# A transformer block on one core: the output projection as seven products of halves, with weight sums kept in DRAM

## The chip, the core and the metric

The kernel runs on one core of a Trainium2 chip. The core has a matrix engine (TensorE, "PE" in the profile; its weight loads are listed apart as "PEld"), a vector engine (VectorE, "DVE"), a scalar engine (ScalarE, "ACT"), GpSimd ("POOL") and a queue that issues transfers (SyncE, "SP"). Each engine works through its own list of instructions in order; the engines wait for each other by semaphores. Matrix products are written to PSUM, eight banks of 128 partitions x 512 float32; everything else lives in SBUF, 128 partitions wide, or in DRAM, reached by DMA. The metric is the device time of one execution in microseconds (us), lower is better. Of the kernel before, three runs are shown beside one profiled execution.

## What is computed

One layer, 512 tokens, model width 2048, 16 heads of 128 (8 stick-breaking, 8 forgetting), inner width 8192, all float32:

```python
h = rmsnorm(x, g_attn)
proj = h @ w_in                              # q, k, v of both kinds of heads, forget gates
o_sb = stick_breaking_attention(qa, ka, va)
o_fox = forgetting_attention(qf, kf, vf, log_f)
mixed = concat(head_rmsnorm(o_sb, g_out_sb), head_rmsnorm(o_fox, g_out_fox))   # (512, 2048)
x = x + mixed @ w_out                        # the output projection, (2048, 2048)
h2 = rmsnorm(x, g_mlp)
x = x + relu(h2 @ w_up) ** 2 @ w_down
y = rmsnorm(x, g_final)
```

## The kernel before

A float32 product is made of three matmuls on split operands. Each operand is split into a high part (a cast on ACT, line 60) and a low part (a subtraction on DVE, line 61); `mm3` (lines 93 to 95) multiplies high by high, high by low and low by high. So each piece of weights costs one pass of ACT, one of DVE, and then PE.

Weights pass through three raw buffers (tag `wraw`, 512 KB each), issued on SP's queue, and then through three pairs of split buffers (`wh`, `wl`, from `hi_lo`). `load_w` does both.

The stages stand in this order. The projections and attention: heads in the order forgetting 6, 7, 0 to 5, then stick-breaking 0 to 7, two heads in a round (`for n in range(0, 2 * NH, 2)`). A round projects q and k of two heads (`project_q`, PSUM tile `accq`), in some rounds v (`accumulate_v`, `accv`), then runs the attention of both at a high priority (`weigh` and the functions that call it; tiles `s`, `pt`, `o`, for the last head `oq`). The normalized head goes to `mixed` (line 265), a tile of 16 heads x 512 tokens; while x is being transposed at the start the same tile holds x, and until the stick-breaking heads come its first eight slices are free.

Output projection (lines 466 to 500): four column blocks `n` of 512. For each, pairs of heads are split again from `mixed` into `uh`, `ul`; 512 KB of `w_out` are loaded and split, and 24 matmuls of 512 columns follow, into four PSUM banks `acco`, one for each block of 128 tokens. Then x is added (line 484), the sum is transposed on PE (line 489) and scaled to `hr` (491), stored to DRAM (`xd`, 492), and the left operands of the next stage are formed and split (`a_form`, lines 449 to 462, tiles `F`, written as `fh` and `fl`); the squares of the row sums go to ACT (line 500).

The up projection and the down projection already use seven products in place of eight for a 2 x 2 product of blocks (a Strassen-Winograd scheme): the sums of the left blocks are `a_form`, those of the right blocks are subtractions in `Unit.product` (lines 547 to 554) and `second`. A unit is a pair of blocks of the inner width; its weights are loaded as two transfers of 1 MB (line 536), for the first unit partly as two of 512 KB (line 531).

The order of instructions on each engine is not the order of the text. A scheduler fixes it when the program is built: it goes through the program with a model of time, takes what is ready in that model, earlier text (or a raised priority) first, and hands out buffers. The chip then keeps that order on each engine and on SP's queue, whatever arrives when. A tile pool that is closed gives its place to later pools; with `reuse_waits="tile"` the later tile waits only for the tiles that lay in its place.

## Time and profile before

| what | value |
|---|---|
| median of three runs | 2092.24 us (2091.91 to 2093.44) |
| profiled execution | 2091.42 us, its span 2089.7 us |
| granted TensorE clock, mean | 0.998 |
| DMA, whole span | 339.68 MB, mean 163 GB/s |
| attention and its projections | to about 658 us |
| output projection, first and last `acco` matmul | 626.0 and 811.4 us |
| up projection starts | 813.35 us |

The profile gives, for one execution, each engine's busy time, the chain of work that ended last (followed back from the last instruction), groups of instructions by source line and tile ("L61 DVE ... wl<-wraw,wh" is line 61 on DVE, which writes `wl` from `wraw` and `wh`), with their count, busy time, mean in ns and the idle time of the engine before them, and on request the same for any stretch of time, in order of time, or by wait. "[0.91 <-DVE fl L61]" behind a row says that the engine was idle 0.91 us before it and what ended that. Busy times of matmuls overlap, since matmuls are pipelined.

### The profile page before, as it was taken

Reading aid. Unit: us, or ns where it says so; the run is one execution under the profiler, and the core shown is the slowest. Engines: PE = TensorE matmul, PEld = TensorE weight load, DVE = VectorE, ACT = ScalarE, POOL = GpSimd, SP = SyncE. Lnnn points to the kernel's source line nnn. Section 1 sums busy time; section 2 is a strip of 40 time slices with the busy share of each in tenths; the row PEclk is TensorE's granted clock in tenths of the full one; section 3 lists DMA queues with packets and bytes.
Section 4 is the critical chain, followed back from the end, with each engine's and each line's share of the span. In section 5 each row is a group of like instructions: output and inputs, shape, how many; then the busy total and the mean of one; then the engine's idle time right before and its main releaser. Section 6 shows DMA issues by size and latency. Waiting matters only on the chain.

```text
span 2089.7 us, 29877 instructions
## 1 busy us (share of the span) xinstructions
PE 2071.5 (99%) x12096; PEld 1842.0 (88%) x12096; DVE 1570.9 (75%) x1746; ACT 1036.4 (50%) x1399; POOL 50.7 (2%) x76
## 2 busy tenths in 40 slices
PE   9999999999999999999999999999999999999998
PEld 8888888888898888999999999999888888888886
DVE  5454545665676666888888888888798888989895
ACT  6333334444445655556665656666743343433443
POOL 0000000000000000000000000000000000000003
PEclk9999999999999999999999999999999999999999
DMA  6333322323323434466566566567856664764732
GB/s 193 81 90 82 85 87 74 88 80 82 81 81 114 157 133 151 137 207 192 182 222 186 186 202 204 182 196 246 298 201 238 232 232 170 288 218 159 264 119 81
DMA packets 239930, 339.68 MB, mean 163 GB/s; under 512 B 7936, under 2 KB 154416, under 8 KB 233776
## 3 DMA queue, kind: packets, MB, share of 16 engines
q1 hardware_dynamic: 238832, 335.64, 49.3%
q8 instruction: 95, 1.56, 0.3%
q10 hardware_dynamic: 960, 2.13, 0.3%
q14 instruction: 43, 0.35, 0.0%
HBM read 272.20 MB, written 65.54 MB: 162 GB/s over the span
## 4 chain that ended last, share of the span: by engine, by line
PE 96%; DVE 2%; DMA 1%; ACT 1%; issue 0%; ACTq 0%; SPq 0%
PE accd L93 7%; PE accd L94 7%; PE accd L95 7%; PE psa L93 6%; PE psa L94 6%; PE psa L95 6%; PE accq L95 6%; PE accq L94 6%; PE accq L93 6%; PE psc L94 3%; PE psc L95 3%; PE psc L93 3%; PE acco L95 3%; PE acco L93 3%; PE acco L94 3%; PE accv L93 3%
## 5 line engine op out<-in xcount | busy, mean ns | idle before, releaser
L60 ACT CAST wh<-wu 128x1024 fp32r<-128x1024 f32 x164 | 171.0, 1048 | 138.7 <-PE psa L94 54.7
L61 DVE TENSOR_TENSOR wl<-wu,wh 128x1024 fp32r<-128x1024 f32 x164 | 199.4, 1221 | 46.5 <-ACT wh L60 46.2
L60 ACT CAST wh<-wd 128x1024 fp32r<-128x1024 f32 (+1 forms) x136 | 134.9, 999 | 184.5 <-PE accd L95 112.8
L61 DVE TENSOR_TENSOR wl<-wraw,wh 128x1024 fp32r<-128x1024 f32 (+2 forms) x133 | 158.6, 1193 | 84.7 <-ACT wh L60 84.1
L93 PE MATMUL psa<-fh,wh 128*128 128x256 f32 x776 | 220.2, 284 | 1.1 <-ACT s L563 1.1
L94 PE MATMUL psa<-fl,wh 128*128 128x256 f32 x776 | 220.0, 284 | 0.9 <-DVE fl L61 0.9
L95 PE MATMUL psa<-fh,wl 128*128 128x256 f32 x776 | 219.8, 283 | 0.0
L60 ACT CAST wh<-wraw 128x1024 fp32r<-128x1024 f32 (+2 forms) x133 | 135.4, 1019 | 154.3 <-PE accq L94 68.5
L93 PE MATMUL accq<-hH,wh 128*128 128x512 f32 x512 | 200.5, 392 | 0.0
L95 PE MATMUL accq<-hH,wl 128*128 128x512 f32 x512 | 200.3, 391 | 0.0
L94 PE MATMUL accq<-hL,wh 128*128 128x512 f32 x512 | 200.2, 391 | 0.0
L61 DVE TENSOR_TENSOR wl<-wd,wh 128x1024 fp32r<-128x1024 f32 (+1 forms) x136 | 155.4, 1153 | 37.6 <-ACT wh L60 37.1
L93 PE MATMUL accd<-wh,uf 128*128 128x512 f32 x436 | 169.7, 389 | 0.9 <-issue 0.9
L94 PE MATMUL accd<-wl,uf 128*128 128x512 f32 x436 | 169.6, 389 | 0.0
L95 PE MATMUL accd<-wh,uf 128*128 128x512 f32 x436 | 169.6, 389 | 0.0
L93 PEld LDWEIGHTS psa<-fh,wh 128*128 128x128 f32 x776 | 149.4, 192 | 1.6 <-ACT s L563 1.3
L94 PEld LDWEIGHTS psa<-fl,wh 128*128 128x128 f32 x776 | 149.3, 192 | 1.2 <-DVE fl L61 1.1
L95 PEld LDWEIGHTS psa<-fh,wl 128*128 128x128 f32 x776 | 149.2, 192 | 0.0
L60 ACT CAST wx<-wd 128x1024 fp32r<-128x1024 f32 (+1 forms) x88 | 87.4, 999 | 114.1 <-PE accd L95 69.9
L61 DVE TENSOR_TENSOR wx<-wd,wx 128x1024 fp32r<-128x1024 f32 (+1 forms) x88 | 100.9, 1152 | 22.9 <-ACT wx L60 22.4
L94 PEld LDWEIGHTS accq<-hL,wh 128*128 128x128 f32 x512 | 96.2, 188 | 19.6
L95 PEld LDWEIGHTS accq<-hH,wl 128*128 128x128 f32 x512 | 96.2, 188 | 19.3
(306 smaller groups left out, 5505.8 us busy)
## 6 DMA issues: line engine op xcount, KB each, us to landing
wu<-in_w_up_dram SPq DMA_DIRECT2D x63, 1024.0 KB, 6.4
ufd<-st SPq DMA_DIRECT2D x98, 512.0 KB, 6.7
wd<-in_w_down_dram SPq DMA_DIRECT2D x48, 1024.0 KB, 6.9
wraw<-in_w_in_dram SPq DMA_DIRECT2D x84, 512.0 KB, 3.7
uf<-ufd SPq DMA_DIRECT2D x42, 1024.0 KB, 7.1
wraw<-in_w_out_dram SPq DMA_DIRECT2D x32, 512.0 KB, 3.5
wd<-in_w_down_dram SPq DMA_DIRECT2D x16, 768.0 KB, 6.8
uf<-ufd SPq DMA_DIRECT2D x14, 768.0 KB, 6.4
```

What stands on the lines that cost most here:

```text
L60: ins = act.copy(hi, src)
L61: lows[0] = dve.tensor_tensor(lo, src, hi.bitcast(F32), op=ALU.subtract)
L93: pe.matmul(out, sh, mh, start=first, stop=False, skip_group_check=True)
L94: pe.matmul(out, sh, ml, start=False, stop=False, skip_group_check=True)
L95: pe.matmul(out, sl, mh, start=False, stop=last, skip_group_check=True)
```

## The change

The output projection becomes seven products of halves too: the 2048 x 2048 weights are cut into 2 x 2 blocks (rows by even and odd head, columns by half), the attention output into 2 x 2 blocks (tokens by half, heads by even and odd).

1. The sums of the weight blocks: in each of the first four rounds of heads, two slices (256 rows of `w_out` each, 2 MB) are loaded into the free half of `mixed`, four subtractions on DVE make the four sums, and 2 MB are stored to DRAM (`wsums`, 16 MB in all). Products 5, 7, 4 and 6 later read their weights there, products 1, 2 and 3 from `w_out`.
2. The left operands `G` of the seven products are formed from `mixed` by the same `a_form` as in the next stage, whole (256 tokens x 8 pairs of heads), in 14 tiles: eight of them lie where the transposed input `hH`, `hL` lay (now eight tiles `h4` in the pool `form1`).
3. For each of two column blocks `db` the products run in the order 1, 2, 5, 6, 7, 3, 4 over four pieces of weights each; sums go into three pairs of PSUM banks A, B, C, and `take` adds them to four quarters of x (`x2`). Products 1 and 2 of the first block begin with the pieces that need no late head (4, 6, 0).
4. A quarter of x that is complete is turned at once (`turn_quarter`); the left operands `F` of the up projection are formed by `left_form` in quarters, in the second block into rooms that `G` has left.
5. At the end of the stage, the weights of units 0 and 1 are loaded, and products 1 and 2 of unit 0 and product 1 of unit 1 are put ahead of the forms that need the last quarter.

The diff, cut to its core:

```diff
+            def sums_of_weights(m):
+                b = mixed[:, :NH].rearrange("p (q a) n -> p q (a n)", a=2)
+                sp.dma_start(b.rearrange("p (s j) c -> p s j c", s=2),
+                             w_out[2 * m * P:2 * (m + 1) * P].rearrange("(s p) (j c) -> p s j c", s=2, j=2))
+                b11, b12, b21, b22 = (b[:, i] for i in range(4))
+                dve.tensor_tensor(b11, b12, b11, op=ALU.subtract)
+                dve.tensor_tensor(b12, b22, b12, op=ALU.subtract)
+                dve.tensor_tensor(b22, b22, b11, op=ALU.subtract)
+                dve.tensor_tensor(b21, b21, b22, op=ALU.subtract)
+                sp.dma_start(wsums[:, m], b)
...
                 qk = [project(0), project(1)]
+                if n < NH:
+                    sums_of_weights(n)
+                    sums_of_weights(n + 1)
...
-    for n in range(4):
-        ns = slice(n * NT, (n + 1) * NT)
-        ps = [acc.tile([P, NT], F32, tag="acc", name="acco") for _ in range(TB)]
...
-            for t in range(TB):
-                ts = slice(t * P, (t + 1) * P)
-                for i in range(2):
-                    mm3(ps[t], ms[i][0][:, ts], ms[i][1][:, ts], *w[i], k0 + i == 0, k0 + i == 2 * NH - 1)
...
+    def g_form(p, m0, m1):
+        a_form(p, mixed[:, 2 * m0:2 * m1].rearrange("p (m s) n -> p m s n", s=2), [g[:, m0:m1, :] for g in G[p]], S_OF[:, m0:m1, :])
+
+    def out_piece(p, db, m0):
+        raw = wp.tile([P, 2, NT], F32, tag="wraw", name="wo")
+        cols = slice(db * NT, (db + 1) * NT)
+        if p in (1, 2, 3):
+            i, j = {1: (0, 0), 2: (1, 0), 3: (1, 1)}[p]
+            sp.dma_start(raw, out_rows[i][:, m0:m0 + 2, j * 2 * NT:(j + 1) * 2 * NT][:, :, cols])
+        else:
+            sp.dma_start(raw, wsums[:, m0:m0 + 2, {5: 0, 7: 1, 4: 2, 6: 3}[p], cols])
+        hi, lo = (w.rearrange("p (a b) -> p a b", a=2) for w in hi_lo(2 * NT))
+        split(hi, lo, raw)
+        ps = {2: B, 5: C, 3: C}.get(p, A)
+        for t in range(2):
+            ts = slice(t * P, (t + 1) * P)
+            for i in range(2):
+                mm3(ps[:, t, :], G[p][0][:, m0 + i, ts], G[p][1][:, m0 + i, ts], hi[:, i, :], lo[:, i, :],
+                    m0 + i == 4 and p in (1, 5, 2), m0 + i == 3)
...
+    def take(p):
+        for q, ps in {1: [((0, 0), A)], 5: [((1, 1), C)], 6: [((0, 1), A)], 2: [((0, 0), B)], 7: [((1, 1), A)],
+                      3: [((0, 1), C)], 4: [((1, 0), A)]}[p]:
+            for t in range(2) if p in (4, 6) else [slice(0, 2)]:
+                dve.tensor_tensor(x2[q][:, t, :], x2[q][:, t, :], ps[:, t, :], op=ALU.add)
...
+    for db in range(2):
+        begin(0, 0, db)
+        if db == 0:
+            for p in (1, 2):
+                g_form(p, 4, 8)
+                g_form(p, 0, 2)
+                for m0 in (4, 6, 0):
+                    out_piece(p, db, m0)
+            for p in (1, 2):
+                g_form(p, 2, 4)
+            for p in (5, 6, 7, 3, 4):
+                g_form(p, 4, 8)
+                g_form(p, 0, 2)
+                g_form(p, 2, 4)
+            mixp_cm.__exit__(None, None, None)
+            rw = ctx.enter_context(tc.tile_pool(name="rw", bufs=5, side="right", reuse_waits="tile"))
+        for i, p in enumerate(G_ORDER):
+            for m0 in (2,) if db == 0 and p in (1, 2) else (4, 6, 0, 2):
+                out_piece(p, db, m0)
...
+            take(p)
+            if db == 1:
+                for q in A_ORDER[2 * i:2 * i + 2]:
+                    for j in range(2):
+                        left_form(q, 0, j)
...
+            if p in (2, 7, 3):
+                turn_quarter(*{2: (0, 0), 7: (1, 1), 3: (0, 1)}[p], db)
+            if db == 1 and p == 6:
+                units = [Unit(u) for u in range(2)]
...
+        if db == 1:
+            begun = [units[0].parts(1), units[0].parts(2)]
+        turn_quarter(1, 0, db)
...
+    for p in (1, 2):
+        units[0].multiply(p, begun[p - 1])
+    units[0].finish(1)
+    begun.append(units[1].parts(1))
+    left_form(4, 1, 0)
+    left_form(5, 1, 0)
+    units[1].multiply(1, begun[2])
+    left_form(6, 1, 0)
+    for p in (7, 3):
+        left_form(p, 1, 1)
+        left_form(p, 1, 0)
```

The pools `acc`, `u`, `att`, `attp` and `mix` get `reuse_waits="tile"`.

## The prediction

> **What bounds the kernel now.** I read the engine totals, then the chain of work that ended last, then busy time by stretch.

> ```profile
> span 2089.7 us, 29877 instructions
> PE 2071.5 (99%) x12096; PEld 1842.0 (88%) x12096; DVE 1570.9 (75%) x1746; ACT 1036.4 (50%) x1399; POOL 50.7 (2%) x76
> PE 96%; DVE 2%; DMA 1%; ACT 1%; issue 0%; ACTq 0%; SPq 0%
> ```

> PE is 96% of the chain, so removed matmuls come off the end as long as everything else stays hidden behind PE. The stretches (columns: length; busy PE, weight loads, DVE, ACT, POOL with counts; clock, DMA share, GB/s):

> ```profile
> 200.00:300.00 100.00, 100.00 (x467) 83.79 (x466) 60.09 (x95) 38.25 (x64) 3.56 (x6) 1.00 0.30 81
> 626.00:680.00 54.00, 54.00 (x259) 45.30 (x258) 37.02 (x50) 28.95 (x46) 0.89 (x2) 1.00 0.34 118
> 680.00:812.00 132.00, 132.00 (x603) 109.39 (x602) 84.54 (x113) 74.22 (x122) 0.00 (x0) 1.00 0.39 132
> 812.00:835.00 23.00, 19.59 (x147) 18.78 (x146) 19.05 (x27) 13.18 (x23) 0.00 (x0) 0.93 0.71 229
> 835.00:850.00 15.00, 15.00 (x127) 15.00 (x127) 11.05 (x11) 8.33 (x11) 0.00 (x0) 1.00 0.46 141
> ```

> The output projection runs from 626 to 812. PE never rests there, and DVE is at (37.02 + 84.54) / 186 = 65%. The one loose stretch is 812 to 835, where the last slice of the residual turns into the up projection's operand: 147 matmuls that take 15 / 127 = 0.118 us each in the next stretch would need 17.4 us, so 5.6 us are lost there.

> **What a matmul costs.** A busy time of 0.39 us is no price, since matmuls overlap. The distance of starts is:

> ```profile
> 799.66 0.39 PE L94 MATMUL acco<-wl,uh 128*128 128x512 f32 x1
> ...
> 811.44 0.40 PE L95 MATMUL acco<-wh,ul 128*128 128x512 f32 x1
> 811.68 1.91 PE L489 MATMUL tr<-ident,x 128*128 128x128 f32 x16
> ```

> From 799.66 to 811.44 lie 52 steps, one row each, so 0.2265 us. The projection has 16 x 4 x 4 x 3 = 768 of them. Seven products of halves need 7 x 2 (token blocks) x 8 (contraction blocks) x 2 (column blocks) x 3 = 672. **The change removes 96 x 0.2265 = 21.7 us of PE.** Transposes stay 64, at 1.91 / 16 = 0.12 us.

> **What the other engines get in exchange.**

> ```profile
> L61 DVE TENSOR_TENSOR ul<-mixed,uh 128x512 fp32r<-128x512 f32 x64 | 43.3, 689 | 38.9 <-PE acco L94 28.1 <-ACT uh L60 10.0 <-PE acco L95 0.8
> L61 DVE TENSOR_TENSOR wl<-wraw,wh 128x1024 fp32r<-128x1024 f32 x25 | 30.6, 1223 | 3.9 <-ACT wh L60 3.9
> L548 DVE TENSOR_TENSOR wu<-wu 128x1024 f32<-128x1024 f32 x31 | 37.8, 1220 | 0.3
> L484 DVE TENSOR_TENSOR x<-x,acco 128x512 f32<-128x512 f32 x16 | 10.9, 684 | 2.8 <-PE acco L95 2.8
> ```

> A piece of weights is still 128x1024 but now feeds 12 matmuls (2.72 us of PE) in place of 24, and there are 56 instead of 32. On DVE the stage then has: 56 low parts x 1.223 = 68.5; the seven left forms of the attention output, each one low part of 1024 and two of 512 (1.22 + 2 x 0.69 = 2.60), 18.2, and four forms with a sum of the same size, 10.4 (in place of 43.3 for the splits of mixed); 14 accumulations into x2 of 1024 columns, 17.2 (before 10.9); the residual's own forms, of 44 operations of 0.69 about 31 before the last turn, 21.4; the last two heads' attention, some 10. Sum 146. PE's stage is 672 x 0.2265 + 64 x 0.12 + some 6 of attention = 166. DVE goes from 65% to 88%: still under PE, without much room.

> *The tail of attention.* Now acco matmuls fill PE while the last head's chain runs:

> ```profile
> 626.00:660.00 34.00, 29.60 (x124) 23.23 (x125) 0.00 (x0) 1.00 0.23 75
> 628.29 1.28 ACT L279 ACTIVATE w<-w 128x1280 f32<-128x1280 f32 x1
> 633.36 1.28 PE L230 MATMUL pt<-ident,w 128*128 128x128 f32 x10
> 636.00 1.49 DVE L61 TENSOR_TENSOR pl<-pt,ph 128x1280 fp32r<-128x1280 f32 x1 [5.56 <-ACT ph L60]
> 641.89 0.39 PE L93 MATMUL oq<-ph,vh 128*128 128x512 f32 x1
> 645.98 0.68 DVE L61 TENSOR_TENSOR pl<-ph,pl 128x512 fp32r<-128x512 f32 x1
> 650.38 0.39 PE L261 MATMUL oq<-pl,onesr 128*128 128x512 f32 x1
> 658.00 0.75 DVE L265 SCALAR_TENSOR_TENSOR mixed<-os_last,g_rest,ph 128x512 f32<-128x512 f32 x1
> ```

> (The first row counts acco alone.) The changed text offers 2 products x 3 pieces x 12 = 72 matmuls that don't need the last heads; then 124 - 72 = 52 are missing, 11.8 us, the upper bound of a hole. But the chain itself is stretched by PE: after the exponent (629.57), the weights' low part (637.49) and the square's (646.66) PE comes 3.8, 4.4 and 3.7 us late, together 11.9. With a shorter PE queue that lateness shrinks, and the hole with it; lower bound 0. I take 3, nearer the lower end, since the two quantities almost cancel. The pt and oq matmuls behind a wait hold up whatever filler stands after them.

> *The burst of forms.* Text order puts five whole left forms (5, 6, 7, 3, 4) ahead of the next pieces: 4 x 5.2 + 2.6 = 23.4 us of DVE, with 1.4 for the late quarters of forms 1 and 2, 8 pieces (9.8) and 4 accumulations (4.9): 39.5 us of DVE while PE has 24 + 48 + 48 matmuls, 27.2 us. Upper bound 12.3. But forms 7, 3 and 4 (13 us) may come later, form chains alternate ACT and DVE so that pieces slip between, and three pieces are split ahead (8.2 us): lower bound 0. I take 4.

> *The piece rate and the loads.*

> ```profile
> wu<-in_w_up_dram SPq DMA_DIRECT2D x63, 1024.0 KB, 6.4
> ufd<-st SPq DMA_DIRECT2D x98, 512.0 KB, 6.7
> uf<-ufd SPq DMA_DIRECT2D x42, 1024.0 KB, 7.1
> wraw<-in_w_out_dram SPq DMA_DIRECT2D x32, 512.0 KB, 3.5
> GB/s 193 81 90 82 85 87 74 88 80 82 81 81 114 157 133 151 137 207 192 182 222 186 186 202 204 182 196 246 298 201 238 232 232 170 288 218 159 264 119 81
> L60 ACT CAST wh<-wraw 128x1024 fp32r<-128x1024 f32 x25 | 26.3, 1050 | 0.0
> ```

> A raw buffer is bound for 3.5 + 1.05 + 1.22, about 6 us, and there are three: one piece every 2 us, against 2.72 needed. 0.52 MB per 2.72 us is 193 GB/s; slices of this trace reach 298. So 0 at best. At worst the four 1 MB loads of the first two units stand in front of pieces: 4 x 6.4 = 25.6 less a reserve of six pieces (16.3) is 9.3. I take 2, since three of four slices after the middle already run at such rates. [...]

> *The sums.* 8 x 4 subtractions of 128x1024 at 1.22 are 39 us of DVE, in the first eight heads, where DVE is at 60%; uncovered they would cost those 39. The 16 transfers of 2 MB pass through SP's queue and the same rings as the projection weights; 6.4 for 1 MB and 3.5 for 0.5 make about 12 for a load. What is queued behind: on DVE the attention's steps behind a subtraction that waits for its load, on SP weight loads behind a store that waits for DVE.

> ```profile
> SPq L83 <- DVE wl L61: 605.9, 113, 10.1
> SPq L492 <- DVE x L484: 8.8, 4, 2.8
> ```

> SP's queue is strictly in order, but the stores of x (L492) stand only 2.2 us each at its head: transfers are queued near the time when their data are ready. I take 1.5, bounds 0 and the slow rival's price below.

> *The turn to the up projection.* Two products of unit 0 and one of unit 1 now run before the last quarter of the residual is turned: 72 x 0.118 = 8.5 us of cover for accumulate, transpose and the next forms. It regains between 0 and 5.6; I take 3, since DVE, 83% busy there, keeps its forms. The regrouped pools (waits for a tile rather than a pool) and the smaller transfers of x: nothing, bounds about 1 us either way.

> **Sum:** -21.7 - 3 + 3 + 4 + 2 + 1.5 = -14.2. The profiled execution took 2091.4 (span 2089.7 and 1.7 around it): 2077.2. The shown median, 2092.2, is 0.8 above that execution, so **2078**.

> **The rivals.** *All covered* (chance 0.17): every loss term is 0, the turn regains all: -27.3, 2065. For it: PE rests nowhere in 626 to 812 now. Against: DVE at 88%.

> *DVE becomes the bound in the first half of the projection* (0.17): hole 8, burst 9, nothing regained at the turn, other terms as above: -21.7 + 8 + 9 + 3.5 = -1.2, 2091, so about no change. For it: 39.5 against 27.2 us above. Against: the slack of forms 7, 3, 4.

> *The sums stand in the in-order queues* (0.16), the slower side. Place: the first eight heads. Each of the eight loads needs some 12 us; if the order of DVE's instructions reckons with a third of that, DVE stands 8 us with the attention chain behind it. PE's lateness of about 4.4 us, as read at the tail, is the cushion; above it PE stands too. 8 x (8 - 4.4) = 29 in place of 1.5: 2078 + 27 = 2105. It decides from 4.4 us of standing. Against: DVE 40% idle, a reserve of three split pieces of 24 x 0.2265 = 5.4 us.

> A hole can cost more than its length:

> ```profile
> 819.37 0.39 PE L94 MATMUL psa<-fl,wh 128*128 128x256 f32 x1 [0.91 <-DVE fl L61]
> 821.57 0.58 PE L93 MATMUL psb<-fh,wh 128*128 128x256 f32 x1 [1.34 <-ACT wh L60]
> 822.17 0.41 PE L94 MATMUL psc<-fl,wh 128*128 128x256 f32 x1
> 822.38 0.41 PE L95 MATMUL psc<-fh,wl 128*128 128x256 f32 x1
> ```

> After idling 0.91 and 1.34 us, a dozen matmuls started 0.21 apart, not 0.12, with the granted clock at 0.93 over the stretch: 1.1 us, inside my bounds. [...]

> **Numbers.** The forecast (2070 to 2086) has 0.50. The range of 2064 to 2101 leaves out most of the slow rival and little else. What can be told from no change is 0.2%, 4.2 us. Faster: 0.50 + 0.17 + 0.06 of the DVE rival = 0.73; same 0.06; slower 0.16 + 0.05 = 0.21.

> **What would show it.** Right: 672 acco matmuls 0.2265 apart, DVE near 88% in that stretch, a few us of PE idle near the last head and after it, less loss at the turn to the up projection, none before 600. Wrong: PE idle in the first eight heads with DVE or SP at a sum (the slow rival); long idle from "wl" or "g" forms in the projection (the DVE rival); acco matmuls further apart.

## The result, and the profile after

The changed kernel takes 2109.38 us (median of 4 runs, 2108.54 to 2110.65) against 2092.09 us (4 runs): 1.0082 times before, 95% interval 1.0064 to 1.0099. It is slower, by 17.3 us, and lies 8 us above the predicted range. The profiled execution took 2108.57 us. Its page of engine totals and chain of waits:

```profile
span 2106.9 us, 29748 instructions
PE 2064.1 (98%) x12000; PEld 1830.2 (87%) x12000; DVE 1626.0 (77%) x1773; ACT 1042.6 (49%) x1396; POOL 52.7 (3%) x76
PE 92%; DVE 5%; ACT 1%; DMA 1%; issue 1%; SPq 0%; ACTq 0%; DVEq 0%
```

There are 96 matmuls fewer (12000 for 12096), as the change says, and PE is busy 7.4 us less; yet the span is 17.2 us longer. PE's share of the chain fell from 96% to 92%, and DVE took 5%: PE now waits. The same stretches as before (length; busy PE, weight loads, DVE, ACT, POOL with counts; clock, DMA share, GB/s) say where:

```profile
200.00:300.00 100.00, 100.00 (x467) 83.76 (x466) 63.76 (x98) 37.99 (x64) 3.28 (x6) 1.00 0.44 132
626.00:680.00 54.00, 42.80 (x174) 33.76 (x174) 42.49 (x52) 27.81 (x37) 0.77 (x2) 0.84 0.36 122
680.00:812.00 132.00, 121.31 (x534) 96.92 (x533) 83.60 (x90) 69.76 (x109) 0.00 (x0) 0.99 0.74 249
812.00:835.00 23.00, 20.22 (x108) 17.51 (x107) 21.45 (x26) 15.85 (x31) 0.00 (x0) 0.93 0.13 52
835.00:850.00 15.00, 12.53 (x97) 11.93 (x96) 14.75 (x22) 8.37 (x12) 0.00 (x0) 0.96 0.01 1
```

In the stretch of the sums (200 to 300) PE is as full as before. From 626 to 850 it rests 54.00 - 42.80 + 132.00 - 121.31 + 23.00 - 20.22 + 15.00 - 12.53 = 27.1 us, where before it rested 3.4; the granted clock from 626 to 680 is 0.84 where it was 1.00; and the transfers between 680 and 812 run at 249 GB/s where they ran at 132.

Idle time leaves out what the lower clock costs. So below, a stretch's *lost* time is the sum, over all starts of matmuls, of the distance to the next start less the distance that such a matmul keeps undisturbed (0.2265 us for 512 columns, 0.118 for 256, 0.112 for a transpose), worked out from the rows of PE. With it the balance closes: from 626 to 870 the kernel lost 6.8 us before and 45.4 us after, 38.6 more; less 96 x 0.2265 = 21.7 that is +16.9, against 17.2 in the spans.

| lost, us | 626-655 | 655-680 | 680-720 | 720-870 | sum | at half clock | time |
|---|---|---|---|---|---|---|---|
| before | 0.1 | 0.1 | 0.1 | 6.6 | 6.8 | 3.4 | 2092.1 |
| after | 6.4 | 12.4 | 11.4 | 15.3 | 45.4 | 27.3 | 2109.4 |
| e3_late | 6.2 | 12.3 | 4.5 | 24.7 | 47.8 | 34.1 | 2112.2 |
| e5_open | 5.9 | 7.7 | 11.0 | 15.5 | 40.2 | 20.5 | 2105.3 |
| e6_pace | 6.5 | 12.4 | 4.8 | 22.0 | 45.6 | 27.3 | 2109.5 |
| e9_half_bytes | 5.9 | 7.8 | 2.7 | 9.4 | 25.9 | 13.7 | 2090.1 |
| e10_open_drip | 6.3 | 7.2 | 3.9 | 11.9 | 29.2 | 13.7 | 2093.3 |
| e14_zeros | 2.1 | 12.1 | 3.8 | 17.0 | 35.0 | 20.5 | 2105.6 |
| e16_prio_seven | 2.6 | 13.3 | 3.7 | 17.3 | 36.9 | 23.9 | 2101.9 |
| e17_pool_forms | 6.3 | 13.2 | 3.6 | 15.4 | 38.4 | 20.5 | 2104.8 |

("At half clock" is the time between 600 and 900 us in which the granted clock was 0.5. In e14_zeros 5 us of added matmuls come on top of the lost time.)

The worst place in the matmuls' own rows (start, busy, engine, line, what; in brackets the idle time before it and who ended it):

```profile
631.20 0.47 PE L98 MATMUL o<-ph,vl 128*128 128x128 f32 x1 [1.98 <-DVE vl L67]
631.48 0.74 PE L96 MATMUL accoa<-wh,g 128*128 128x512 f32 x1
632.01 0.63 PE L97 MATMUL accoa<-wl,g 128*128 128x512 f32 x1
632.44 0.63 PE L98 MATMUL accoa<-wh,g 128*128 128x512 f32 x1
...
657.08 0.39 PE L98 MATMUL accoa<-wh,g 128*128 128x512 f32 x1
663.45 0.80 PE L96 MATMUL accob<-wh,g 128*128 128x512 f32 x1 [5.99 <-ACT g L63]
...
665.75 0.80 PE L98 MATMUL accob<-wh,g 128*128 128x512 f32 x1 [1.07 <-DVE g L64]
...
672.69 0.50 PE L98 MATMUL accoc<-wh,g 128*128 128x512 f32 x1 [1.46 <-DVE g L64]
```

Product 1 starts at 631.48, behind the o matmuls of the head before the last (before, the projection started at 626 between them). By 657.08 the matmuls that don't need the last head are used up, and PE rests 5.99 us until that head's form is there; two short waits for forms (g) follow. VectorE's rows tell when that head was done:

```profile
662.00 0.75 DVE L271 SCALAR_TENSOR_TENSOR mixed<-os_last,g_rest,ph 128x512 f32<-128x512 f32 x1
662.67 1.82 DVE L500 TENSOR_TENSOR s<-mixed 128x1024 f32<-128x1024 f32 x2
```

The last write of `mixed` starts at 662.00 (before: 658.00), and only behind it the sums of form 5 (L500), then those of forms 7, 6 and 3. In steps of 3.41 us the granted clock (the number behind the five engines) answers:

```profile
654.37:657.79 3.42, 3.10 (x14) 2.24 (x12) 1.74 (x2) 1.29 (x2) 0.00 (x0) 1.00 0.54 158
657.79:661.20 3.41, 0.00 (x0) 0.00 (x0) 2.72 (x4) 1.97 (x3) 0.00 (x0) 1.00 0.53 163
661.21:664.62 3.41, 1.17 (x2) 0.50 (x2) 3.34 (x6) 1.84 (x3) 0.00 (x0) 0.50 0.94 336
664.63:668.03 3.40, 2.33 (x6) 1.84 (x6) 3.40 (x5) 3.40 (x6) 0.00 (x0) 0.50 0.78 265
668.04:671.44 3.40, 3.19 (x8) 2.00 (x6) 3.40 (x6) 2.54 (x4) 0.00 (x0) 0.50 0.00 0
671.46:674.86 3.40, 2.17 (x9) 1.80 (x10) 3.40 (x5) 0.00 (x1) 0.00 (x0) 1.00 0.02 5
```

The step after the empty one is at 0.50, and so are the two after it: 10.2 us in which matmuls of 512 columns start 0.43 us apart, as 632.01 and 632.44 above do. The second bad place is the loads: SP's own rows, then ScalarE's (its first operation on a piece of weights):

```profile
692.71 3.58 SPq L517 DMA_DIRECT2D wu<-in_w_up_dram  x3
696.39 3.23 SPq L588 DMA_DIRECT2D wo<-wsums  x1
699.66 0.64 SPq L517 DMA_DIRECT2D wu<-in_w_up_dram  x1
...
702.93 1.05 SPq L517 DMA_DIRECT2D wu<-in_w_up_dram  x1
```

```profile
706.31 1.04 ACT L63 CAST wh<-wo 128x1024 fp32r<-128x1024 f32 x1 [9.41 <-DMA wo<-wsums]
710.36 1.04 ACT L63 CAST wh<-wo 128x1024 fp32r<-128x1024 f32 x1 [3.00 <-DMA wo<-wsums]
715.45 1.05 ACT L63 CAST wh<-wo 128x1024 fp32r<-128x1024 f32 x1 [4.05 <-DMA wo<-in_w_out_dram]
```

Five loads of 1 MB (two units of the up projection and half of the third) are issued between pieces of 0.5 MB, and ScalarE stands 9.41, 3.00 and 4.05 us for a piece. It starts on the piece issued at 696.39 at 706.31, 9.9 us later; the median landing time of these pieces over the whole run is 3.9 us.

### The profile page after: what moved, and what is told of

Same layout as the page of the kernel before. It is cut to its first block, busy times and chain, and to the rows that moved or that the text cites. A ratio compares the mean times of both kernels' runs of the same rounds, so it can differ in the third digit from the quotient of the medians.

```text
span 2106.9 us, 29748 instructions
## 1 busy us (share of the span) xinstructions
PE 2064.1 (98%) x12000; PEld 1830.2 (87%) x12000; DVE 1626.0 (77%) x1773; ACT 1042.6 (49%) x1396; POOL 52.7 (3%) x76
## 4 chain that ended last, share of the span: by engine, by line
PE 92%; DVE 5%; ACT 1%; DMA 1%; issue 1%; SPq 0%; ACTq 0%; DVEq 0%
PE accd L96 7%; PE accd L98 7%; PE accd L97 7%; PE psa L96 6%; PE psa L97 6%; PE psa L98 6%; PE accq L98 6%; PE accq L96 6%; PE accq L97 6%; PE psc L98 3%; PE psc L97 3%; PE psc L96 3%; PE accv L96 2%; PE accv L97 2%; PE accv L98 2%; PE psb L97 1%
## 5 line engine op out<-in xcount | busy, mean ns | idle before, releaser
L64 DVE TENSOR_TENSOR wl<-wu,wh 128x1024 fp32r<-128x1024 f32 x168 | 204.4, 1222 | 47.8 <-ACT wh L63 46.7
L96 PE MATMUL psa<-f,wh 128*128 128x256 f32 x768 | 218.3, 284 | 0.5 <-ACT s L556 0.5
L97 PE MATMUL psa<-f,wh 128*128 128x256 f32 x768 | 218.1, 284 | 0.0
L98 PE MATMUL psa<-f,wl 128*128 128x256 f32 x768 | 218.0, 284 | 0.0
L63 ACT CAST wh<-wraw 128x1024 fp32r<-128x1024 f32 (+2 forms) x101 | 101.7, 1008 | 157.0 <-PE accq L97 80.8
L64 DVE TENSOR_TENSOR wl<-wraw,wh 128x1024 fp32r<-128x1024 f32 (+2 forms) x101 | 119.2, 1181 | 56.1 <-ACT wh L63 56.1
L96 PEld LDWEIGHTS psa<-f,wh 128*128 128x128 f32 x768 | 148.1, 193 | 0.7 <-ACT s L556 0.7
L97 PEld LDWEIGHTS psa<-f,wh 128*128 128x128 f32 x768 | 147.9, 193 | 0.0
L98 PEld LDWEIGHTS psa<-f,wl 128*128 128x128 f32 x768 | 148.0, 193 | 0.0
L64 DVE TENSOR_TENSOR wx<-wd,wx 128x1024 fp32r<-128x1024 f32 (+1 forms) x89 | 102.6, 1161 | 23.9 <-ACT wx L63 23.6
L96 PE MATMUL accd<-wx,uf 128*128 128x512 f32 x288 | 112.2, 390 | 1.1 <-ACT wx L63 1.1
## 6 DMA issues: line engine op xcount, KB each, us to landing
wu<-in_w_up_dram SPq DMA_DIRECT2D x64, 1024.0 KB, 6.8
ufd<-st SPq DMA_DIRECT2D x98, 512.0 KB, 6.9
wd<-in_w_down_dram SPq DMA_DIRECT2D x48, 1024.0 KB, 6.7
wraw<-in_w_in_dram SPq DMA_DIRECT2D x84, 512.0 KB, 3.8
uf<-ufd SPq DMA_DIRECT2D x42, 1024.0 KB, 6.3
wo<-wsums SPq DMA_DIRECT2D x32, 512.0 KB, 3.9
```

The costliest lines, as they stand in the source:

```text
L63: ins = act.copy(hi, src)
L64: lows[0] = dve.tensor_tensor(lo, src, hi.bitcast(F32), op=ALU.subtract)
L96: pe.matmul(out, sh, mh, start=first, stop=False, skip_group_check=True)
L97: pe.matmul(out, sh, ml, start=False, stop=False, skip_group_check=True)
L98: pe.matmul(out, sl, mh, start=False, stop=last, skip_group_check=True)
```

## The experiments

e17 and e18 are timed; the others are single executions beside one of before on the same chip (2092.1 to 2092.9 us). Lost time is from the table above.

**The sums.** e1_nosums leaves out the making of the sums; products 5, 7, 4 and 6 read blocks of the weights themselves in their place.

```diff
-                if n < NH:
-                    sums_of_weights(n)
-                    sums_of_weights(n + 1)
```

> The weight sums are left out (no load, no subtraction, no store), and products 5, 7, 4 and 6 read blocks of w_out in their place, so their weights are not the sums. Theory: the sums beside the first heads cost nothing, since PE loses 8.7 us in the first 600 us both before and after the change; then the time stays within 2 us of the changed kernel's 2109, with the same idle times after 626. Rival (my slow one): the sums' transfers and subtractions disturb the attention; then several us come back before 600. Second rival: pieces read from the kept sums come later than pieces from w_out; then the waits on pieces near 706 shrink and the time falls by 3 to 8 us.

2109.29 us: the sums cost nothing, and the slow rival of the prediction falls. (Lost time before 600 us, too, is 12.7 us before the change and after it.)

**The late start, first tries.** e2_swap exchanges the PSUM banks of A and B; e4_freetail does not write the last two heads to `mixed`, so nothing of the projection waits for them.

```diff
-... for c in "abc")
+... for c in "bac")          # e2: A lies where B lay
-            dve.scalar_tensor_tensor(mixed[:, h, :], os_, gv, va, ...)
+            to = os_ if left < 2 and h < NH and h >= NH - 2 else mixed[:, h, :]
+            dve.scalar_tensor_tensor(to, os_, gv, va, ...)
```

> PSUM pairs A and B change places: A now lies in the two banks that the last q and k leave at 600, B in the two that v holds until 631. Theory: the idle 2.6 us at 627 to 631 arise because product 1 finds no free bank, and they bring the half clock at 630 to 637; then product 1 starts near 610 to 626, both vanish and 5 to 6 us of the 6.4 lost there come back, though a hole just before the last head may grow by the filler used up: 2103 to 2108 in all. Rival: v itself is late and PE has nothing to do there anyway; then nothing changes.

> The last two heads' results are written to their own tile instead of mixed, so the left forms do not wait for them (two slices of the projection's operand are stale). Theory: the hole of 6.0 us before the last head and most of the burst of left forms behind it (waits on g at 664 to 687, half clock 661 to 671) are the price of the last heads' lateness; then 10 to 18 us come back, 2091 to 2099. Rival: the forms are a price of DVE's amount of work alone; then the hole goes but the waits on g stay, and only 5 to 8 us come back.

2108.58 and 2111.08 us: both missed. In e2 the first accoa matmul still starts at 631.81. In e4 PE waits 6.08 us for g at 666.23 and 5.85 at 673.30: the sums of form 5 start at 663.88, right behind the last head's own last step at 663.21, although no data hold them. Their room (`s12`) and the banks of C come out of pools that open only when attention is through; e7_open_early below, which takes the room of `s12` from elsewhere, has sums of forms by 628 us, but C's first matmul still waits for the last head (658.02).

**The pool.** e5_open gives A and B buffers of the pool of q, k and v, which stays open, as the accumulators before the change had them.

```diff
-    acc_cm.__exit__(None, None, None)
...
-    aps, bps, cps = (ops.enter_context(tc.tile_pool(name=f"{c}ps", ...)) for c in "abc")
-    A, B, C = (q.tile([P, 2, NT], F32, name=f"acco{c}") for c, q in zip("abc", (aps, bps, cps)))
+    A, B = ([acc.tile([P, NT], F32, tag="acc", name=f"acco{c}") for _ in range(2)] for c in "ab")
+    C = ops.enter_context(tc.tile_pool(name="cps", ...)).tile([P, 2, NT], F32, name="accoc")
```

> Edit: the accumulators of products 1 and 2 come out of the PSUM pool of q, k and v, which stays open, instead of out of pools that open only when attention is through; nothing else. Theory A (depth): what is missing beside the last heads is not the early start but matmuls. A bank now takes one product of 8 blocks, 24 matmuls x 0.2265 = 5.4 us, where before it took 16 heads, 48 matmuls = 10.9 us; ahead of the last two heads there are 72 matmuls = 16.3 us in four banks, where before there were 168 = 38.1 us. Product 1 then starts near 626 us instead of 631.5 us, the half clock at 630 us goes, but the matmuls run out some 5 us sooner and the hole ahead of 662 us grows by as much: 2109 us within 2, and a hole of 9 us or more near 660 us. Theory B (late start): the start behind the last o matmuls cost the 6.4 us lost between 626 and 655 us, and they come back: 2103 us.

2105.32 us, between the two. PE's waits from 620 to 680 us, one of 0.23 us left out:

```profile
655.66 0.79 PE L96 MATMUL accoa<-wh,g 128*128 128x512 f32 x1 [5.03 <-ACT g L63]
667.55 0.79 PE L98 MATMUL accoc<-wh,g 128*128 128x512 f32 x1 [3.47 <-DVE g L64]
```

The waits among the o matmuls are gone and the last head is done 5 us sooner (656.80), but a hole stays, though not the 9 us that theory A asked for. It ends with the form of the head before the last, whose write of `mixed` starts at 654.21 (647.24 in the changed kernel). Fewer matmuls stand beside the last heads: a bank takes 24 matmuls of one product, 5.4 us, and three quarters of that in four banks are 16.3 us, where before 168 matmuls, 38 us, stood beside the last two heads.

**The loads.** e3_late ties the unit loads behind the last piece of product 6 of the second round; e6_pace issues them one at a time at four places, and the third unit's behind the last piece.

```diff
+                with tc.issue_after(issued[0].ins):      # e3
                     units = [Unit(u) for u in range(2)]
...
+    AT = {(0, 7): (0, 0), (0, 4): (0, 1), (1, 2): (1, 0), (1, 6): (1, 1)}      # e6
...
+            if (db, p) in AT:
+                u, half = AT[db, p]
+                units[u].load(half)                      # issue_after the last piece so far
```

> The loads of the first units (five of 1 MB, issued at 692 to 703 between the pieces) are tied behind the last piece of product 6 of the second column block. Theory: they stand ahead of pieces and cost the waits at 704.8 to 716.5 (2.2 + 0.8 + 0.8 us) and the half clock at 709; then 5 to 6 us come back, 2103 to 2105, and nothing else moves. Rival: pieces are late there because DVE has spent its time on the left forms; then the waits stay and the time changes by less than 1 us.

> Edit: the four 1 MB loads of the first two units of the up projection are issued one at a time, behind the last piece of products 7 and 4 of the first round and 2 and 6 of the second, instead of all together behind product 6 of the second round's order; the third unit's behind the last piece. Theory (bursts of loads): five loads in a row stood ahead of the pieces between 692 and 704 us, and one at a time they do not: the loss between 680 and 720 us falls from 11.4 us to under 6 and is not given back later: 2103 us, 2100 to 2106. Rival (the queue has no room for them): the loss only moves to where the loads stand now, as when they were tied behind product 6: 2108 to 2113 us.

2112.24 and 2109.49 us. In both, the loss between 680 and 720 fell (11.4 to 4.5 and 4.8), and came back where the loads now stand. In e3_late:

```profile
791.09 0.79 PE L96 MATMUL accoa<-wh,g 128*128 128x512 f32 x1 [8.59 <-ACT wh L63]
```

So in both tries 1 MB loads in front of pieces make PE wait where they stand. e9_half_bytes (on e5) then leaves out the loads of half of the pieces; e10_open_drip leaves all the bytes, cuts the loads of units 0 and 1 and spreads them, and, as e6_pace does, moves the third unit's behind the last piece:

```diff
+        if m0 in (6, 2) and (p, db) not in ((1, 0), (2, 0)):     # e9, on e5
+            raw = last_raw[0]                                    # no load
...
+        count[0] += 1                                            # e10, on e5: in out_piece
+        if todo and count[0] % 2 == 0:
+            u, half, q = todo.pop(0)
+            units[u].load(half, q)       # 0.25 MB: a = slice(2 * q, 2 * q + 2), issue_after this piece
```

> Edit: on e5_open; of the pieces of the weights of the output projection every second one is not loaded: two pieces in a row are split from the same 0.5 MB, so that the loads of these products are half of the bytes (the products are then not those of the reference). Theory (rate of loads): a product is 48 matmuls = 10.9 us and wants four pieces of 0.5 MB, 193 GB/s, where before 192 matmuls = 43.5 us wanted 4 MB, 96 GB/s; with the five 1 MB loads of the up projection on top nothing is left in hand, so at half of the bytes the waits for wh and wl go: of the 26.5 us lost between 680 and 870 us at least 10 come back, 2093 to 2096 us. Rival (work on VectorE and ScalarE is what is late): the splits stay as many, and the time falls by less than 3 us: 2102 to 2106 us.

> Edit: e5_open, with the loads of the first two units of the up projection cut into sixteen of 0.25 MB, one behind every second piece. Theory (a 1 MB load ahead of a piece is what makes the piece late): 0.625 MB for each 2.72 us of matmuls is 230 GB/s, no piece comes more than a microsecond late, and the loss between 680 and 820 us falls from 15.9 to 8: 2097 us, 2094 to 2100. Rival (the rate itself is too high): it stays within 2 us of e5_open, 2103 to 2107 us.

2090.09 and 2093.25 us, 15.2 and 12.1 less than e5_open. The stretch from 680 to 812, for e5_open, e9_half_bytes and e10_open_drip:

```profile
680.00:812.00 132.00, 121.55 (x535) 96.72 (x534) 82.87 (x93) 68.81 (x107) 0.00 (x0) 0.99 0.75 246
```

```profile
680.00:812.00 132.00, 128.08 (x580) 103.72 (x579) 93.08 (x106) 76.93 (x122) 0.00 (x0) 1.00 0.48 162
```

```profile
680.00:812.00 132.00, 126.49 (x572) 102.27 (x571) 89.83 (x100) 73.63 (x117) 0.00 (x0) 1.00 0.75 247
```

At half of the bytes PE rests 3.9 us instead of 10.5; with the same mean rate (247 GB/s) but no load of 1 MB between the pieces it rests 5.5. Most of it is how the loads stand in the queue, not the mean rate: the rival of e10 falls, and e9 wins only 3.2 us more. Moving the third unit's load alone can't be what won, since e6_pace does it too and won nothing. By the median of e10_open_drip's repetition below (2095.16) the gain is 10.2 us, not 12.1.

**VectorE behind the last heads.** Six runs try to give PE its forms sooner. e7_open_early (on e5) takes the room of the forms' sums from an earlier head's q and k, so that the forms may start ahead; e11_open_spread (on e5) makes the forms two products ahead of their use; e13_prio (on e10) gives form 5, the last take and the last turn priority; e8_all7, e12_all and e15_prio_alt combine such edits with an exchange of products 5 and 6.

```diff
-    S_OF = xp.tile([P, NH, 2 * P], F32, tag="hr1", name="s12")
+    S_OF = [up.tile([P, 2, 2 * P], F32, tag=t_, name="s12") for t_ in ("uh0", "ul0", "uh1", "ul1")]  # e7, e8
...
+            for q in {5: (5, 6), 6: (7,), 7: (3, 4)}.get(p, ()) if db == 0 else ():   # e11; in e12 with 5 and 6 exchanged
+                g_form(q, 4, 8)  ...
...
+                with tc.high_priority() if p == 5 else ExitStack():                   # e13, e15
...
-    G_ORDER = (1, 2, 5, 6, 7, 3, 4)
+    G_ORDER = (1, 2, 6, 5, 7, 3, 4)                                                   # e8, e12, e15
```

> Edit: as e5_open, and the room for the sums of the left blocks is that of q and k of an earlier head, so that forms 5, 6, 7, 3 and 4 of the heads that are ready need not wait for the end of attention. Theory (burst of forms): behind the hole the matrix engine waited four times for forms (5.99, 1.07, 1.46 and 1.60 us) and ran 10.2 us at half clock; with 3/4 of the forms done ahead the waits behind the first go, and the loss between 655 and 720 us falls from 23.8 to 12 to 15 us: 2098 to 2102 us. Rival (order on VectorE): forms that VectorE does ahead of the last head's own work make that head later, and the hole grows by what the burst loses: 2108 to 2112 us.

> Edit: e7_open_early and e6_pace together, products 5 and 6 exchanged in order (so that two products in a row never use the same banks), and products 1 and 2 taken to 7/8 of their depth ahead of the last two heads, not to 3/4 (84 matmuls = 19.0 us instead of 72 = 16.3 us). If the parts found so far are each real and add (about 6 at the loads, 9 at the burst, 3 at the reuse of banks, 2.7 at the depth): 2087 us, 2083 to 2093. If the missing depth decides and the rest only moves with it: 2100 us or more.

> Edit: e5_open, with forms 5 to 4 made two products ahead of their use and not all in one burst. Theory (VectorE's queue in the burst): takes and splits of pieces no longer stand behind forms that nobody wants yet; the waits for g (3.47 us) and for the take of product 6 (1.73 us) and part of the half clock go: 2100 us, 2097 to 2103. Rival (the hole ahead of the last head's end and the loads decide): 2104 to 2107 us.

> Edit: e10_open_drip and e11_open_spread together, and products 5 and 6 exchanged in order so that no product writes the banks of the one ahead of it. If the parts add (8 for the loads, 5 for the burst, 3 for the banks): 2089 us, 2086 to 2094. If they only move one another: 2098 us or more.

> Edit: e10_open_drip, with form 5 (and the last take and turn) ahead of whatever else is ready on VectorE. Theory (order on VectorE): behind the last heads VectorE made the sums of form 7 ahead of the remainders of form 5, for which the matrix engine waited 3.56 us; that wait falls under 1.5 us, and of the 2.8 us at the turn half goes: 2090 us, 2088 to 2092. Rival (VectorE has as much to do in any order): the wait comes back at product 6, 2092 to 2095 us.

> Edit: e13_prio, with products 5 and 6 exchanged in order, so that product 6 is followed by one that writes other banks, and the first turn of the first round one product later. Theory (reuse of banks): the two waits for a take of product 6 (1.34 and 1.41 us) go: 2.5 to 4 us less than e13_prio. Rival (the take moves ahead of something else on VectorE, as in e12_all): no less than e13_prio.

2113.86, 2116.36, 2106.01, 2104.28, 2096.23 and 2103.18 us: none gains on what it was built on (e5_open 2105.32, e10_open_drip 2093.25 and, timed below, 2095.16). In e7_open_early forms made ahead stand before the last head's own steps, and the weights' transposes wait:

```profile
638.45 2.40 PE L236 MATMUL pt<-ident,w 128*128 128x128 f32 x10 [2.98 <-POOL w L228]
```

In e8_all7 that wait is 6.04 us, and product 6 waits 14.47 us for the take of product 1. That take comes behind the forms and then behind a load of x, for which VectorE itself stands 4.88 us (3.03 in e7_open_early): in these two runs the pool of x opens later, so they are no pure test of the order of forms. In e12_all and e15_prio_alt PE stands 9.46 and 8.86 us at 671 for the take ahead of a transpose. In the runs that leave x alone, something of VectorE's is late there whichever way the work is ordered; busy time from 655 to 680 in e10_open_drip:

```profile
655.00:680.00 25.00, 21.44 (x83) 17.11 (x83) 25.00 (x33) 15.86 (x25) 0.00 (x0) 0.84 0.44 148
```

And in the kernel before:

```profile
655.00:680.00 25.00, 25.00 (x118) 20.74 (x117) 16.52 (x22) 11.99 (x21) 0.00 (x0) 1.00 0.48 168
```

VectorE is busy 25.00 of 25.00 us, where it was 16.52, and PE isn't. By this it is the bound of this stretch; no run with less work on it, at its usual speed, shows what that would win.

**The hole filled.** e14_zeros adds 22 matmuls of a zero tile ahead of it; e16_prio_seven (on e13) gives PE 12 useful ones there, by splitting the last piece of products 1 and 2 between the heads 4, 5 and 6, 7.

```diff
+                for i in range(22 if p == 1 else 0):      # e14
+                    pe.matmul(A[i % 2][:16, :], zero, G[1][0][:, 4:6, :]..., start=False, stop=False, ...)
...
+                g_form(p, 2, 3)                           # e16
+                out_piece(p, db, 2, rest[p])              # only its first contraction block; the second later
```

> Edit: e10_open_drip, with 22 matmuls of a zero tile (5.0 us at full clock, they add nothing to the sums) between the pieces of product 1 and of product 2 that stand ahead of the last two heads. Theory (clock): the hole of 5.03 us ahead of 655 us is filled with work that is worth nothing, so only what follows the hole can be won: the half clock from 652.5 us on (6.8 us, so 3.4 us lost) goes, and the time falls by 2 to 4 us: 2090 us, 2089 to 2091.5. Rival (the half clock costs nothing there, or the matmuls stand in front of the attention): 2093 to 2098 us.

> Edit: e13_prio, with products 1 and 2 taken to 7/8 of their depth ahead of the last two heads (84 matmuls = 19.0 us instead of 72 = 16.3 us). Theory (depth): the hole of 5.03 us becomes 2.3 us, and with the forms ahead of it on VectorE nothing is given back: 2 to 4 us less than e13_prio. Rival (form 5 is what the matrix engine waits for next, and it comes no sooner): within 1 us of e13_prio.

2105.59 and 2101.86 us: both missed. The loss ahead of 655 us fell (6.3 to 2.1 and 2.6), that from 655 to 680 rose by 4.9 and 6.1, and that from 720 on by some 5 more (in e16, which is built on e13_prio, by 3 against that run). e16_prio_seven:

```profile
653.97 0.50 PE L96 MATMUL accoa<-wh,g 128*128 128x512 f32 x1 [2.08 <-ACT g L63]
659.11 0.50 PE L96 MATMUL accob<-wh,g 128*128 128x512 f32 x1 [3.49 <-ACT g L63]
...
667.76 0.80 PE L98 MATMUL accoc<-wh,g 128*128 128x512 f32 x1 [4.34 <-DVE g L64]
```

PE now waits 2.08, 3.49 and 4.34 us for forms, where e10_open_drip waits 5.03 and 3.56. The last head itself is later; its write of `mixed` in e10_open_drip, then in e14_zeros:

```profile
655.85 0.75 DVE L271 SCALAR_TENSOR_TENSOR mixed<-os_last,g_rest,ph 128x512 f32<-128x512 f32 x1
659.91 0.75 DVE L272 SCALAR_TENSOR_TENSOR mixed<-os_last,g_rest,ph 128x512 f32<-128x512 f32 x1
```

With 5.0 us of matmuls more it starts 4.1 us later; with 2.7 us more (e16 against e13_prio) 2.0 us later (657.87 against 655.91). The added matmuls stand in PE's list ahead of the last head's own (its first oq matmul on `pl` starts at 653.59 in e14_zeros, at 648.52 in e10_open_drip), as e14's rival feared, so most of the filled hole comes back as a later last head. That depth alone is the cause of the hole, as theory A has it, isn't shown.

**VectorE relieved by GpSimd.** e17_pool_forms (on e10) gives GpSimd the sums and remainders of form 7 and the remainders of form 4.

```diff
-            dve.tensor_tensor(a21, a11, a21, op=ALU.subtract)
+            eng.tensor_tensor(a21, a11, a21, op=ALU.subtract)    # eng = pool for p in (7, 4), in split too
```

> Edit: e10_open_drip, with the sums and remainders of form 7 and the remainders of form 4 made by GpSimd, which has nothing to do there, instead of VectorE. Theory (VectorE's work behind the last heads): VectorE made 4.5 us of form 7 between the sums of form 5 and its remainders; without it form 5 is there some 4 us sooner, the wait of 3.56 us falls under 1 us, and the half clock that follows it may go too; GpSimd takes 1.29 us for 512 columns, so 15.5 us for its 12 pieces, and is done by 675 us, ahead of product 7 near 688 us: 2089 us, 2086 to 2091. Rival (VectorE and GpSimd get in each other's way, or a later wait takes the place of this one): 2092 to 2096 us.

2104.77 us (4 runs; 1.0065 times before, 1.0048 to 1.0082): the rival's cause, and more than its 2092 to 2096. VectorE's sums of form 5, its remainders and a take, first in e10_open_drip, then in e17_pool_forms, with GpSimd's own rows last:

```profile
656.51 2.42 DVE L499 TENSOR_TENSOR s<-mixed 128x1024 f32<-128x1024 f32 x3
...
663.53 0.68 DVE L620 TENSOR_TENSOR x<-x,accoa 128x512 f32<-128x512 f32 x1
...
665.33 2.43 DVE L64 TENSOR_TENSOR g<-s,g 128x1024 fp32r<-128x1024 f32 x3
```

```profile
656.24 4.64 DVE L500 TENSOR_TENSOR s<-mixed 128x1024 f32<-128x1024 f32 x3
...
663.58 1.27 DVE L621 TENSOR_TENSOR x<-x,accoa 128x512 f32<-128x512 f32 x2
664.77 4.59 DVE L64 TENSOR_TENSOR g<-s,g 128x1024 fp32r<-128x1024 f32 x3
```

```profile
657.55 2.79 POOL L504 TENSOR_TENSOR mixed<-mixed 128x1024 f32<-128x1024 f32 x1 [25.34 <-DVE s L500]
660.29 2.82 POOL L64 TENSOR_TENSOR g<-mixed,g 128x1024 fp32r<-128x1024 f32 x1
```

While GpSimd worked, these sums and remainders of VectorE, with both inputs in SBUF, took about twice their time (2.42 to 4.64, 2.43 to 4.59 us for three), the single remainder of 512 columns between them four times (0.69 to 2.85); the takes, with an input in PSUM, kept theirs (0.68, and 1.27 for two). What was taken off VectorE is paid back: form 5's remainders start 0.56 us sooner, where 4 us were hoped for.

**The best version, timed.** e18_drip_timed is e10_open_drip again.

> Edit: none; e10_open_drip again, timed, as the best of the runs with seven products. If its one look was typical: 2093 us, ratio to before 1.000 to 1.001, so that the loads and the pools together give back the 17 us and the 21.7 us of matmuls are spent to the last microsecond on what is left between 626 and 870 us. If its short turn to the up projection (2.6 us lost behind 820 us, where nine other runs lose 8 to 11) was luck of one execution: 2097 to 2100 us.

2095.16 us (11 runs, 2093.52 to 2100.96), 1.0016 times before, 1.0007 to 1.0025. So the loads and the pool give back some 14 of the 17.3 us, and no complete version with all seven products, of those run, beats the kernel before.

## Why the prediction was wrong

Point by point, by its own terms:

- *96 matmuls, -21.7:* right. 672 acco matmuls, 0.227 us apart where nothing waits, and the balance above closes with them.
- *The sums, +1.5 (and the rival at 2105):* measured 0 (e1_nosums). The time came out near that rival's by luck, for other reasons.
- *The piece rate and the loads, +2 (0 to 9.3): with the tail, the step that failed most.* Cutting and spreading the loads won 10 to 12 us (e10_open_drip and its repetition against e5_open). The prediction had named the place, the 1 MB loads in front of pieces, and then reckoned with a reserve of six pieces, 16.3 us, and took 2 because other stretches run at such rates. The reserve wasn't there: when ScalarE had to wait 9.41 us for a raw piece, PE started 27 more matmuls (6.1 us) from the end of ScalarE's last cast at 696.91 on, and went idle for 2.18 us ahead of 707.41. The mean rate said little (249 GB/s in the slow stretch, 247 in the mended one); how the loads stand in the one queue decided.
- *The tail of attention, +3 (0 to 11.8):* two waits among the o matmuls (0.61 and 1.98 us) and 5.99 us of hole, 8.6 us idle, and half clock from 630 to 637 and from 661 us on. The step that failed is "the two quantities almost cancel": a shorter queue on PE was to bring the last head's chain forward by as much as the missing matmuls are long. But the chain came 4 us later, at 662.00, with product 1 held behind the o matmuls of the head before. PE's lateness, which was to shrink from 11.9 us (3.8, 4.4 and 3.7), grew to 16.0 at the same three places (7.9, 4.1 and 4.1). With the pool mended (e5_open) the lateness is 8.4 us (4.1, 4.4 and 0) and the chain comes sooner than before, by 1.2 us (656.80), but not by the 11.8 that are missing, and a hole of 5 us remains. A shorter PE queue does make the chain less late, but here by 3.5 us, where a hole of 3 out of 11.8 reckoned with some 9; and half the contraction per product halves what a bank can take in advance.
- *The burst of forms, +4 (0 to 12.3):* behind the hole 1.07, 1.46 and 1.60 us of waits, with the half clock (661 to 671) some 8 us. The slack that was to soften it, forms 7, 3 and 4 later, was not used: the order fixed at build puts form 7's sums and remainders between form 5's sums and its remainders, which start at 671.42, 4 us after ScalarE had finished its part of them (667.38). That stretch is the prediction's rival of VectorE as the bound, for 25 us of the projection, while its 65% to 88% was reckoned over the whole.
- *The turn to the up projection, -3:* wrong in sign. From 720 to 870 the loss rose by 8.7 us, of which 4 lie at the turn itself, from 812 on (10.6 against 6.6), the rest in the second round of the products. With the loads cut 5.3 stay (11.9 against 6.6), but only about 1 at the turn (7.7), so nothing was regained there. PE stands 1.56 us for a form and 1.26 us for a take at the transposes, and later 1.79 us for a remainder (rows below); e13_prio, which was to mend the first two, still lost 7.8 there. The other 4 us lie between 720 and 780, among them 1.41 us for a take (778.20) and 0.86 ahead of transposes; what causes them stays open.
- *The clock, "inside my bounds":* it wasn't. Half clock rose from 3.4 to 27.3 us, worth up to (27.3 - 3.4) / 2 = 12 us of matmuls. It is no term of its own, since it follows each hole; but each hole term should have carried it.

PE's waits at the turn in e10_open_drip:

```profile
814.50 0.42 PE L631 MATMUL tr<-ident,x 128*128 128x128 f32 x2 [1.56 <-ACT f L63]
816.19 1.43 PE L631 MATMUL tr<-ident,x 128*128 128x128 f32 x6 [1.26 <-DVE x L620]
835.03 0.39 PE L98 MATMUL psa<-f,wx 128*128 128x256 f32 x1 [1.79 <-DVE wx L64]
```

What stays open: whether less work on VectorE between 655 and 680 us would make seven products the faster way. e14_zeros and e16_prio_seven show that filling PE's hole ahead of the last head's own matmuls doesn't, and e17_pool_forms that handing forms 7 and 4 to GpSimd doesn't. Having ScalarE take part of the sums, or doing only the second round by seven products (so that the first keeps the deep accumulators beside the last heads), wasn't tried.

## What to carry to other kernels

Products of halves save matmuls and halve the contraction that one accumulator takes; so they halve the independent work that can stand beside a late producer, and double the loads per matmul. Before such a change, count in matmuls what is left to hide the last producer's chain and the other queue users, and price each hole with the clock that follows it (here 27.3 us at half clock where there were 3.4). Where two sizes of load share one in-order queue, cut the large one and spread it between the small ones: here 16 loads of 0.25 MB in place of 4 of 1 MB were worth 10 to 12 us at the same mean rate (246 and 247 GB/s from 680 to 812 us).

## What the runs showed of the hardware

*VectorE beside GpSimd.* GpSimd's last row behind the heads in e17_pool_forms starts at 668.78 and lasts 8.94 us, to 677.72. VectorE's remainder of a piece of weights (`wl<-wo,wh`, 128x1024) took 2.78 us at 672.12, and 1.21 us from 678.20 on; its takes of 512 columns took 0.67 us at 671.52 and 0.68 at 676.50.

*The kept sums.* Each partition's kept sums lie 128 KiB behind those of the one before in DRAM. A piece of 0.5 MB of them landed in 3.9 us in the run after, and so did the 24 pieces of 0.5 MB that come from the weights themselves (columns: queue, count, KB each, us to landing):

```profile
mixed<-in_w_out_dram SPq DMA_DIRECT2D x8, 2048.0 KB, 9.0
wsums<-mixed SPq DMA_DIRECT2D x8, 2048.0 KB, 7.7
wo<-wsums SPq DMA_DIRECT2D x32, 512.0 KB, 3.9
```
